# Two layers of a hybrid diffusion backbone on one core: sums of weights issued one step a unit, four columns at the head of the up-projection, and first products that take latents before context

## The chip, the cores and the metric

The kernel runs as one program on one core of a Trainium2 chip. A core has a matrix engine (TensorE, PE in the profile, with its weight loads shown as PEld), a vector engine (VectorE, DVE), an activation engine (ScalarE, ACT), a general engine (GpSimd, POOL) and a synchronising engine (SyncE, SP). SP, ACT and POOL can each issue transfers (DMA), and each issues in its own order. The metric is the device time of one execution in microseconds, the median of several runs.

## The reference, cut to what matters

512 latent tokens and 256 context tokens of width 1024 pass two layers in float32. `setup_inputs` draws the weights; the shapes are those of the constants.

```python
for l in range(DEPTH):                                  # 2
    sh1, sc1, g1, sh2, sc2, g2 = split(silu(c) @ w_ada[l] + b_ada[l], 6)   # for context: c_ctx
    h  = modulate(rms_norm(x,  norm1_g[l]), sh1, sc1)
    hc = modulate(rms_norm(xc, norm1_g[l]), csh1, csc1)
    glu, q, k, v, rq, rk, rv, rg, gates = split(h @ w_in[l] + b_in[l])     # and of hc
    a   = conv_module(glu)                              # depthwise, 31 taps, layer norm, silu
    att = latent_attention(q, k, v, k_c, v_c)           # 8 heads, 2 kv heads
    ret = retention_output(bidir_retention(rq, rk, rv), rg)
    x = x + g1 * (merge_branches(gates, a, att, ret) @ w_out[l])
    x = x + g2 * conv_ffn(modulate(rms_norm(x, norm2_g[l]), sh2, sc2), w_up[l], w_down[l])
    # context tokens: the same weights, not in the last layer
return rms_norm(x, final_norm_g)
```

## The kernel before, in words

Activations lie with features on the partitions and the 768 tokens in the free dimension. Every large product is done in three matmuls: an operand is split into a rounded part `hi` (ACT, line 218 for weights) and a rest `lo` (DVE, line 219), and hi*hi, hi*lo and lo*hi are added up in PSUM. Weights come as tiles of 128 x 1024 through `Stream`: SP loads them into six raw buffers, ACT and DVE split them at most four tiles ahead. Of the eight PSUM banks, four belong to the pool `pd` (`dps()`) and four to `ps` (`ps()`). Nearly all SBUF tiles come from one pool of 45 slots (`S()`); a new tile waits until what used its slot before is done, a transfer included.

The first layer starts in `start` and `first_products`. SP loads x in eight tiles, then the columns of `w_ada` for the first shift and scale in pieces listed by `START` (column, width, number of weight tiles loaded by then). A piece goes through three stages: `go(0, c0)` its matmuls, `go(1, c0)` two transposes and copies on DVE, `go(2, c0)` a small folding matmul and eight small additions on DVE. Piece by piece the normalised, modulated blocks `hh`, `hl` of 128 features become ready (`modulated1`, `modulated2`), and `products` multiplies each by two units of weights (keys and values, then the first queries). Inside `start` the order of PE, ACT and DVE is the order of the code.

A layer's mixers then run by `ORDER`, a list of units: K and Q (keys, queries), R (retention values), A (starts attention, which runs on beside the units), G (glu, for the convolution, which C starts), P (the other retention inputs), T (gates). Attention goes over four pairs of heads and six token tiles; a pair's output `att` is spilled to memory by `spill` after its last tile, and the retention that follows loads the table `ij` into a slot and makes its decay tables of it (lines 916 and 930).

The first layer's up-projection takes seven products in place of eight for each two-by-two block of `w_up` and of the tokens (`up_seven`, `up_order`). For this, sums of weight blocks are needed: S1 = 21 + 22, S3 = 11 + 21, S2 = 11 + S1, S4 = 12 + S2. `make_sums` lets transfers do them: for each of six batches of columns POOL issues four copies in memory and four accumulating transfers, 1 MB each (half of that in the last batch). The first copy of a sum waits for the last matmul that was written out at that point; `SUMAT` names the six units after which one batch each is issued.

Between mixers and up-projection, `last_chunks` does the last four row blocks of `w_out` once for the second half of the tokens and once for the first, and between its chunks steps the generator of `split_tokens`, which normalises the half that is done and makes the operands "11" and "12" of it. The operands S2, S1, S3, 22, S4 need both halves; `up_seven` steps the generator again for them. So that PE has work until "S2" is there, the products "11" and "12" of the first `UPFIRST` columns come first.

Of the kernel before, what the change touches and what calls it, by code (L numbers as in the profile page):

```python
# [18 lines left out]
F32 = mybir.dt.float32  # L19
# [6 lines left out]
P = 128  # L26
# [12 lines left out]
NSUB = 140  # L39
START = ((0, 256, 2), (256, 256, 0), (512, 256, 4), (768, 256, 0))  # L40
ND = 4
# [8 lines left out]
ATTR, RETR, CONVR, ADAR = (1.0, 1.0), (1.4, 1.6), (0.4, 0.4), (0.06, 0.28, 0.4, 0.33)  # L50
SUMAT = ("R1", "G1", "G2", "G3", "P1", "P2")
QLAG = 2
# [6 lines left out]
PEP, DVP, LATE = (4,), (2, 3), (5,)  # L59
NADA = 24 + 8 * len(PEP)  # L60
ROWS = 1552
# [35 lines left out]

UPFIRST = 3
CUTS = ((0, 4), (4, 8), (8, 12), (12, 16), (16, NFF))
# [3 lines left out]
def up_order():  # L103

    first = range(UPFIRST)
    out = [(n, c) for c in first for n in ("11", "12")] + [(n, c) for n in ("S2", "S1", "S3") for c in first]
    for c in range(UPFIRST - 1):
        out += [("22", c), ("S4", c)]
    for c in range(UPFIRST, NFF):
        out += [("11", c), ("22", c - 1), ("S4", c - 1)]  # L110
        if c in CUTAT:
            out.append((CUTAT[c],))
        out += [("12", c), ("S2", c), ("S1", c), ("S3", c)]
    return out + [("22", NFF - 1), ("S4", NFF - 1)]
# [170 lines left out]
class Kern:  # L285
# [92 lines left out]

    def last_chunks(self, key, xs, segs, hold, evac, norm, lead=0, limit=None):

# [23 lines left out]
        for i, hs in enumerate(halves):  # L404
            for j, m in enumerate(range(KC - hold, KC)):
                evac(m, self.dense(None, xs, hs, ws[j]))
                if i == len(halves) - 1:
                    ws[j] = None
                    self.W.release(tiles[j + 1])
                if gen:  # L410
                    for _ in range(1 + KC // hold):
                        next(gen, None)
                self.tick(self.cost)
# [206 lines left out]

    def make_sums(self, b):

        n = len(batches()[b]) * Q
        src = {x: self.io[f"wup{4 * b + i}"] for i, x in enumerate(BLOCKS)}
        for name, base, more in SUMS:
            t = src[name] = self.up_sums[b][name] = self.dram.tile([P, n], F32, name=f"sum{name}_{b}")
            first = self.nc.gpsimd.dma_start(t, src[base], max_dma_last_dim=2048)

            info = mybir.DependencyInfo(mybir.DependencyClass.Sync, mybir.DependencyReason.DATA)
            self.tc.add_manual_dep(first.ins, self.last_mm.ins.name, info, reason="later")  # L630
            for x in more:
                self.nc.gpsimd.dma_start(t, src[x], accum_op=ALU.add, max_dma_last_dim=2048)


    def rstd2(self, pts, name, y=None):
# [501 lines left out]
    def first_products(self, xs, ada):  # L1137
# [9 lines left out]

        def products(k, units=(0, 1)):
            for u in units:
                wh, wl = wb[u][k % 4]  # L1150
                for t in range(n):
                    pt = banks[u][t // 2][:, 256 * (t % 2):256 * (t % 2) + 256]
# [3 lines left out]

        def weights(c):
            self.W.limit = 2 * c + 2
            return [[self.W.next(("w_in", 0, k * P, col), 256) for k in range(4 * c, 4 * c + 4)] for col in (1536, 1024)]

# [5 lines left out]

        for k in range(KC):
            self.sq_add(k, xs[k], ALL, k == KC - 1)
        r = self.S("rstd")
        self.sq_rstd(ALL, r)  # L1170
        go(0, 0)
        go(1, 0)
        go(2, 0)
        banks = [[self.dps() if ND > 3 * u + v else self.ps() for v in range(n // 2)] for u in range(2)]
        t0 = m1(0)
        wb = weights(0)
        m2(t0, 0)
        t1 = m1(1)
        go(0, 256)
        go(1, 256)  # L1180
        m2(t1, 1)
        products(0)
        go(2, 256)
        t2 = m1(2)
        products(1)
        t3 = m1(3)
# [9 lines left out]
        m2(t4, 4)  # L1196
        wb = weights(1)
        go(0, 768)
# [297 lines left out]
    def spill(self, dst, t, w):  # L1496
        self.nc.gpsimd.dma_start(dst[:, :w], t[:, :w])

# [56 lines left out]
    def layer_mixers(self, l, last, segs, T, xs, xsp, first, h2):  # L1555
# [16 lines left out]
        def mixers():  # L1572
# [9 lines left out]
            self.ij = self.S("ij")  # L1582
            nc.gpsimd.dma_start(self.ij[:, :4 * P + 2], io["ij"])
            self.ret_tables()
# [8 lines left out]
        ths, merged = [], [None] * KC  # L1593
        for step in ORDER[l].split():
            kind, i = step[0], int(step[1:] or 0)
# [16 lines left out]
            elif kind == "T":  # L1612
                ths.append(self.gate(2, len(ths), segs))
            if l == 0 and step in SUMAT:
                self.make_sums(SUMAT.index(step))
        self.finish(mix)
# [28 lines left out]
        def evac(m, pts):  # L1645
            for pt, o, c in kinds(pts):
# [6 lines left out]
        return self.last_chunks(lambda m, k: ("w_out", l, k * P, m * P), mm, even(segs), HOLDO[l], evac, norm, LEADO,  # L1653
                                None if l else NUP + UPFIRST)

    def ffn(self, l, h2, xs, segs, T, gen, xsp, xup):
# [57 lines left out]
        def up_seven():  # L1714
# [37 lines left out]
            def s1(c):  # L1752
                Z[c] = (self.ps() if 0 < c < UPFIRST else self.dps())[:, :HALF]
                product(Z[c], "S1", c)
# [29 lines left out]
            for n, x in enumerate(up_order()):  # L1784
# [8 lines left out]
                elif x[0] != "S2" or x[1] >= UPFIRST:  # L1793
                    steps[x[0]](x[1])
                if n == 0:
                    next(gen)
# [194 lines left out]
```

## Time and profile before

| what | value |
|---|---|
| median of 3 runs | 2313.04 us (2312.16 to 2316.35) |
| profiled execution | 2318.38 us |
| its span, first to last instruction | 2316.6 us |
| busy: PE, DVE, ACT, POOL | 96%, 69%, 43%, 6% |
| mean granted clock of PE | 0.988 of 2.4 GHz |
| moved by DMA | 307 MB |

The profiled execution lies 5.3 us above the median of the runs. PE's busy time says only that a matmul was under way; a clock below 1.0 means that matmuls took longer.

### The profile page before, as it was taken

What the parts mean: (1) busy time and instruction counts of PE and PEld (TensorE: products, weight loads), DVE (VectorE), ACT (ScalarE), POOL (GpSimd) and SP (SyncE); (2) the same over time, 40 slices, a digit from 0 to 9 for tenths busy, and PEclk for the clock granted to TensorE, in tenths of its full rate; (3) what the DMA queues carried; (4) which work ended last, traced back from release to release, by engine and by line L of the source; (5) the groups of instructions that cost most, each with busy time, mean ns of one, the idle gap of its engine ahead of it and who ended that gap; (6) DMA issues with size and microseconds to landing.
All of it is one profiled execution on the core that took longest, in us unless ns stands there. A gap on an engine that the chain in (4) does not pass through costs nothing.

```text
span 2316.6 us, 34409 instructions
## 1 busy us (share of the span) xinstructions
PE 2232.2 (96%) x13386; PEld 2037.1 (88%) x13386; DVE 1604.8 (69%) x3219; ACT 989.0 (43%) x1707; POOL 144.5 (6%) x225
## 2 busy tenths in 40 slices
PE   6999968999999989999999989999999999999998
PEld 5988958999999989999999979888887889888887
DVE  6876936889985567565655669878699756744445
ACT  3465643342242346554454434565343434423233
POOL 0001111100010000101101100000001100000000
PEclk9999989999999999999999999999999999999999
DMA  8226894813343333737647521111126623432221
GB/s 304 101 99 173 232 243 126 216 64 117 129 156 128 106 103 100 182 119 191 153 152 183 184 109 56 58 55 58 55 80 222 252 84 111 159 113 97 100 91 37
DMA packets 104466, 307.03 MB, mean 133 GB/s; under 512 B 11024, under 2 KB 13344, under 8 KB 104304
## 3 DMA queue, kind: packets, MB, share of 16 engines
q1 hardware_dynamic: 66240, 186.34, 23.5%
q0 software_dynamic: 38064, 118.50, 18.9%
q8 instruction: 105, 1.72, 0.3%
q14 instruction: 57, 0.47, 0.1%
HBM read 282.26 MB, written 68.68 MB: 151 GB/s over the span
## 4 chain that ended last, share of the span: by engine, by line
PE 53%; issue 3%; DVE 3%; DMA 1%; ACT 1%; POOL 0%; DVEq 0%; POOLq 0%; ACTq 0%
PE pd L319 31%; PE pd L1724 11%; PE ps L319 8%; PE ps L1724 2%; PE ps L1378 1%; DVE wlo L219 1%; DMA crow<-crow 0%; DMA rowa<-wadt 0%; ACT whi L218 0%; DVE cacc L827 0%; DMA rl<-attsp 0%; DVE qq L1326 0%; ACT dx L1805 0%; DMA raw<-wstream 0%; DVE rowa L599 0%
## 5 line engine op out<-in xcount | busy, mean ns | idle before, releaser
L218 ACT ACTIVATE whi<-raw 128x1024 fp32r<-128x1024 f32 x313 | 331.4, 1061 | 748.0 <-PE pd L319 492.0
L219 DVE TENSOR_TENSOR wlo<-raw,whi 128x1024 fp32r<-128x1024 f32 x313 | 382.3, 1222 | 258.8 <-ACT whi L218 245.1
L319 PE MATMUL pd<-hh,whi 128*128 128x384 f32 (+2 forms) x1472 | 471.1, 360 | 0.0
L319 PE MATMUL pd<-hh,wlo 128*128 128x384 f32 (+2 forms) x1472 | 470.2, 359 | 0.0
L319 PE MATMUL pd<-hl,whi 128*128 128x384 f32 (+2 forms) x1472 | 469.5, 359 | 0.0
L319 PEld LDWEIGHTS pd<-hh,whi 128*128 128x128 f32 x1472 | 270.9, 188 | 28.0 <-issue 1.8
L319 PEld LDWEIGHTS pd<-hh,wlo 128*128 128x128 f32 x1472 | 271.4, 188 | 25.9 <-issue 1.1
L319 PEld LDWEIGHTS pd<-hl,whi 128*128 128x128 f32 x1472 | 271.2, 188 | 25.9 <-issue 0.7
L827 DVE SCALAR_TENSOR_TENSOR cacc<-u,vec,cacc 128x497 f32<-128x497 f32 (+9 forms) x360 | 220.9, 650 | 2.0
L1724 PE MATMUL pd<-hh,whi 128*128 128x384 f32 x512 | 171.8, 339 | 9.1 <-ACT hh L716 9.1
L1724 PE MATMUL pd<-hl,whi 128*128 128x384 f32 x512 | 172.3, 336 | 0.5 <-DVE hl L717 0.4
L1724 PE MATMUL pd<-hh,wlo 128*128 128x384 f32 x512 | 171.7, 336 | 0.0
L1361 ACT ACTIVATE prob<-ps,amx,qrs 128x256 f32<-128x256 f32 (+1 forms) x144 | 93.8, 656 | 91.3 <-DVE amx L1356 74.9
L319 PE MATMUL pd<-whi,hl 128*128 128x256 f32 x416 | 120.3, 290 | 5.9 <-DVE hl L784 5.9
L319 PE MATMUL pd<-whi,hh 128*128 128x256 f32 x416 | 120.3, 292 | 2.1 <-ACT hh L781 2.1
L319 PE MATMUL pd<-wlo,hh 128*128 128x256 f32 x416 | 119.3, 287 | 0.0
L319 PE MATMUL pd<-hidh,whi 128*128 128x512 f32 (+1 forms) x302 | 104.1, 356 | 4.0 <-DVE x L1814 4.0
L1724 PEld LDWEIGHTS pd<-hh,whi 128*128 128x128 f32 x512 | 96.5, 189 | 12.0 <-ACT hh L716 10.1
L319 PE MATMUL pd<-hidl,whi 128*128 128x512 f32 (+1 forms) x302 | 103.1, 353 | 0.0
L319 PE MATMUL pd<-hidh,wlo 128*128 128x512 f32 (+1 forms) x302 | 102.9, 354 | 0.0
L599 DVE SCALAR_TENSOR_TENSOR rowa<-rowa,crow 128x768 f32<-128x768 f32 (+1 forms) x144 | 94.4, 686 | 8.9 <-DMA rowa<-wadt 8.9
L588 POOL DMA_DIRECT2D rowa<-wadt x72 | 39.1, 543 | 950.1 <-DVE wlo L219 737.1
(298 smaller groups left out, 4312.1 us busy)
## 6 DMA issues: line engine op xcount, KB each, us to landing
raw<-wstream SPq DMA_DIRECT2D x236, 512.0 KB, 3.5
rowa<-wadt POOLq DMA_DIRECT2D x72, 512.0 KB, 4.3
sumS<-wup POOLq DMA_DIRECT2D x30, 1024.0 KB, 13.0
raw<-sumS SPq DMA_DIRECT2D x88, 256.0 KB, 3.7
raw<-wup SPq DMA_DIRECT2D x66, 256.0 KB, 3.6
xup<-dx POOLq DMA_DIRECT2D x32, 384.0 KB, 7.2
sumS<-sumS POOLq DMA_DIRECT2D x10, 1024.0 KB, 9.7
adar<-wada SPq DMA_DIRECT2D x16, 384.0 KB, 7.6
```

Source lines behind the costliest of these rows:

```text
L218: nc.scalar.activation(hi, r, AF.Copy)
L219: nc.vector.tensor_tensor(lo, r, hi.bitcast(F32), op=ALU.subtract)
L319: self.last_mm = self.nc.tensor.matmul(out, w, x, start=start, stop=stop)
L588: nc.gpsimd.dma_start(loaded[-1], self.io["wadt"][l, 8 * pc + c])
L599: nc.vector.scalar_tensor_tensor(out, raw[:, a:b], 1.0, t[:, o:o + b - a], op0=ALU.mult, op1=ALU.mult, accum_out=acc[:, c, j, h:h + 1])
L827: nc.vector.scalar_tensor_tensor(acc[:, a:b], u[:, a + d:b + d], w(k), acc[:, a:b], op0=ALU.mult, op1=ALU.add)
L1361: nc.scalar.activation(pr[:, o - k0:o - k0 + c], pt[:, :c], AF.Exp, scale=rs, bias=mx[:, 2:3], accum_out=sm[:, j:j + 1])
L1378: nc.tensor.transpose(pt[:, b * P:b * P + P], pr[:, o + b * P:o + b * P + P], self.ident)
L1724: nc.tensor.matmul(pt, w[:, b], x, start=start and k == 0 and i == 0, stop=k == 3 and i == 2, skip_group_check=not start)
```

## The change

`START` begins with two pieces of 128 columns in place of one of 256. `first_products` makes the sum of squares, the reciprocal root and the first block separately for latents and for context, and the first unit's products of the latents come before everything of the context. `make_sums(n)` is called after every unit from the ninth on (G1) and issues for each batch the step that is its turn: the copies, then S1 and S3, then S2, then S4; every transfer of a step waits for the last matmul written out. `spill` issues on ACT instead of POOL, the load of `ij` on SP instead of POOL. `UPFIRST` becomes 4, all products "11" come before all "12", Z of all four columns lies in `ps`, the generator is stepped after the second product, and `PACE` steps it 3, 3, 1 and 1 times behind the four last chunks.

```diff
-START = ((0, 256, 2), (256, 256, 0), (512, 256, 4), (768, 256, 0))
+START = ((0, 128, 2), (128, 128, 0), (256, 256, 4), (512, 256, 0), (768, 256, 0))
-SUMAT = ("R1", "G1", "G2", "G3", "P1", "P2")
+SUMFROM = 8
-UPFIRST = 3
+PACE = (3, 3, 1, 1)
+UPFIRST = 4
-    out = [(n, c) for c in first for n in ("11", "12")] + [(n, c) for n in ("S2", "S1", "S3") for c in first]
+    out = [(n, c) for n in ("11", "12", "S2", "S1", "S3") for c in first]
...
-                    for _ in range(1 + KC // hold):
+                    for _ in range(pace[j] if pace else 1 + KC // hold):
...
-    def make_sums(self, b):
...
+    def make_sums(self, n):
+        steps = ((), ("S1", "S3"), ("S2",), ("S4",))
+        for b in range(len(batches())):
+            if not 0 <= n - b < len(steps):
+                continue
+            for name, base, more in SUMS:
+                if n == b:
+                    t = sums[name] = self.dram.tile([P, len(batches()[b]) * Q], F32, name=f"sum{name}_{b}")
+                    ops.append(nc.gpsimd.dma_start(t, src[base], max_dma_last_dim=2048))
+                elif name in steps[n - b]:
+                    for x in more:
+                        ops.append(nc.gpsimd.dma_start(sums[name], src[x] if x in src else sums[x], accum_op=ALU.add,
+                                                       max_dma_last_dim=2048))
+            for op in ops:
+                self.tc.add_manual_dep(op.ins, self.last_mm.ins.name, info, reason="later")
...
-        for k in range(KC):
-            self.sq_add(k, xs[k], ALL, k == KC - 1)
-        r = self.S("rstd")
-        self.sq_rstd(ALL, r)
-        go(0, 0)
+        for k in range(KC - 1):
+            self.sq_add(k, xs[k], ALL)
+        for seg in ALL:
+            self.sq_add(KC - 1, xs[KC - 1], [seg])
+        for (o, c), in (lat, ctx):
+            y.append(self.ps()[:, :c])
+            self.mm(y[-1], self.ones, self.sq[:, o:o + c], True, True)
+            if o == 0:
+                go(0, 0)
         go(1, 0)
+        self.rstd2([(y[0], *lat[0])], "rstd", r)
         go(2, 0)
...
+        t0 = self.modulated1(0, xs[0], r, 0, 0, lat)
+        wb = [weights(0, 0)]
+        self.modulated2(0, t0, 0, 0, lat, h0)
+        wb.append(weights(0, 1))
+        products(0, (0,), th)
+        self.rstd2([(y[1], *ctx[0])], "rstd", r)
+        t0 = self.modulated1(0, xs[0], r, 0, 0, ctx)
+        self.modulated2(0, t0, 0, 0, ctx, h0)
+        go(0, 128)
+        products(0, (1,), th)
+        go(1, 128)
+        products(0, (0,), tc)
+        go(2, 128)
         t1 = m1(1)
+        products(0, (1,), tc)
+        m2(t1, 1)
         go(0, 256)
         go(1, 256)
-        m2(t1, 1)
-        products(0)
+        products(1, (0,))
         go(2, 256)
         t2 = m1(2)
-        products(1)
+        products(1, (1,))
...
     def spill(self, dst, t, w):
-        self.nc.gpsimd.dma_start(dst[:, :w], t[:, :w])
+        self.nc.scalar.dma_start(dst[:, :w], t[:, :w])
...
-            nc.gpsimd.dma_start(self.ij[:, :4 * P + 2], io["ij"])
+            nc.sync.dma_start(self.ij[:, :4 * P + 2], io["ij"])
...
-            if l == 0 and step in SUMAT:
-                self.make_sums(SUMAT.index(step))
+            if l == 0 and n >= SUMFROM:
+                self.make_sums(n - SUMFROM)
...
-                Z[c] = (self.ps() if 0 < c < UPFIRST else self.dps())[:, :HALF]
+                Z[c] = (self.ps() if c < UPFIRST else self.dps())[:, :HALF]
...
-                if n == 0:
+                if n == 1:
                     next(gen)
```

## Rows read from the trace of the kernel before

**Rows 1.** The page: span, and each engine's busy time.

```profile
span 2316.6 us, 34409 instructions
PE 2232.2 (96%) x13386; PEld 2037.1 (88%) x13386; DVE 1604.8 (69%) x3219; ACT 989.0 (43%) x1707; POOL 144.5 (6%) x225
```

**Rows 2.** PE's waits over the span: total us, times, longest.

```profile
PE ps L319 <- ACT probt L1379: 23.9, 1, 23.9
...
PE pd L1724 <- ACT hh L716: 9.1, 3, 6.7
```

**Rows 3.** Windows: each engine's busy us, granted clock, DMA share, GB/s.

```profile
327.90:351.80 23.90, 0.01 (x2) 0.01 (x2) 0.00 (x0) 0.45 (x3) 4.26 (x6) 0.56 0.96 253
351.80:355.00 3.20, 3.20 (x20) 2.87 (x21) 0.00 (x0) 1.21 (x5) 1.24 (x3) 0.53 0.68 95
361.40:364.90 3.50, 0.05 (x3) 0.03 (x1) 2.47 (x7) 3.50 (x10) 0.00 (x0) 1.00 0.00 0
364.90:370.00 5.10, 5.10 (x30) 4.82 (x31) 3.65 (x7) 0.22 (x1) 0.00 (x0) 0.67 0.00 0
```

**Rows 4.** Timeline of ACT and POOL: start, us, instruction, idle before and releaser.

```profile
296.02 0.30 ACT L1393 ACTIVATE att<-ps 128x128 f32<-128x128 f32 x1
...
337.75 0.96 POOL L1497 DMA_DIRECT2D attsp<-att  x1
...
351.35 0.38 ACT L1379 ACTIVATE probt<-ps 128x256 f32<-128x256 f32 x1 [24.87 <-DMA attsp<-att]
351.50 0.99 POOL L1583 DMA_DIRECT2D ij<-ij  x1
```

**Rows 5.** Timeline behind the stall; weight loads 232 to 327 (ns min/median/max, first, last).

```profile
361.00 0.49 ACT L916 ACTIVATE kdec<-lg,ij 128x8 f32<-128x8 f32 x2 [6.91 <-DMA ij<-ij]
...
364.90 1.59 PE L319 MATMUL ps<-rq,rk 64*128 64x128 f32 x8 [3.45 <-DVE kb L981]
...
L199 SPq DMA_DIRECT2D raw<-wstream x7: 327/328/328, 236.5 to 320.3; - x7
```

**Rows 6.** Transfers issued 232 to 327: size, median us to landing.

```profile
raw<-wstream SPq DMA_DIRECT2D x7, 512.0 KB, 7.3
attsp<-att POOLq DMA_DIRECT2D x1, 384.0 KB, 13.2
```

**Rows 7.** The second load of `ij`; sums, by tile (first and last start).

```profile
1583.16 0.54 POOL L1583 DMA_DIRECT2D ij<-ij  x1 [5.24 <-PE ps L1378]
...
L632 POOL DMA_DIRECT2D sumS<-sumS x12: 874/1042/1440, 194.4 to 456.1; - x12
...
L197 SPq DMA_DIRECT2D raw<-sumS x88: 319/327/922, 800.7 to 1285.1; - x88
```

**Rows 8.** Timeline at the up-projection's head; last row: one product in the chain.

```profile
849.92 0.61 DVE L1648 SCALAR_TENSOR_TENSOR x<-pd,coef,x 128x384 f32<-128x384 f32 x1
...
855.68 0.51 ACT L657 ACTIVATE sqt<-x 128x384 f32<-128x384 f32 x1
...
858.40 0.55 DVE L1737 TENSOR_TENSOR fg<-fg,ps 128x384 f32<-128x384 f32 x1
...
860.27 1.22 DVE L219 TENSOR_TENSOR wlo<-raw,whi 128x1024 fp32r<-128x1024 f32 x1
...
869.16 1.33 PE L1724 MATMUL pd<-hh,whi 128*128 128x384 f32 x3 [6.66 <-ACT hh L716]
...
875.78 0.45 PE L1724 MATMUL pd<-hh,whi 128*128 128x384 f32 x1 [1.15 <-ACT hh L716]
...
901.00 2.08 PE ps L1724 x12
```

**Rows 9.** The start: a wait of PE, a piece's matmuls, matmuls with ones.

```profile
PE pd L319 <- DVE hl L784: 4.5, 2, 2.3
...
24.10 2.52 PE L319 MATMUL ps<-adar,cc 128*32 128x256 f32 x32
...
L319 PE MATMUL ps<-sqt,ones 128*128 128x512 f32 x2 | 1.9, 1061 | 0.0
```

More of the change, by code (lines that the diff above doesn't have):

```diff
@@ L59 @@
 PEP, DVP, LATE = (4,), (2, 3), (5,)
-NADA = 24 + 8 * len(PEP)
+NADA = 26 + 8 * len(PEP)
 ROWS = 1552
@@ L377, in dense, with last_chunks @@
         return pts
-    def last_chunks(self, key, xs, segs, hold, evac, norm, lead=0, limit=None):
+    def last_chunks(self, key, xs, segs, hold, evac, norm, lead=0, limit=None, pace=None):
         n = len(xs)
@@ L619, in up_operand @@
         return t[:, j * Q:j * Q + Q]
-    def make_sums(self, b):
[L623 to L632, printed above, removed]
+    def make_sums(self, n):
+        nc = self.nc
+        info = mybir.DependencyInfo(mybir.DependencyClass.Sync, mybir.DependencyReason.DATA)
+        steps = ((), ("S1", "S3"), ("S2",), ("S4",))
+        for b in range(len(batches())):
+            if not 0 <= n - b < len(steps):
+                continue
+            sums = self.up_sums[b]
+            src = {x: self.io[f"wup{4 * b + i}"] for i, x in enumerate(BLOCKS)}
+            ops = []
+            for name, base, more in SUMS:
[8 more added lines that the diff above has]
+                self.tc.add_manual_dep(op.ins, self.last_mm.ins.name, info, reason="later")
     def rstd2(self, pts, name, y=None):
@@ L1146, in go, with products @@
                     next(part)
-        def products(k, units=(0, 1)):
+        def products(k, units=(0, 1), ts=range(n)):
             for u in units:
                 wh, wl = wb[u][k % 4]
-                for t in range(n):
+                for t in ts:
                     pt = banks[u][t // 2][:, 256 * (t % 2):256 * (t % 2) + 256]
@@ L1155, in products, with weights @@
                         self.mm(pt, x, y, k == 0 and i == 0 and t % 2 == 0, k == KC - 1 and i == 2 and t % 2 == 1)
-        def weights(c):
-            self.W.limit = 2 * c + 2
-            return [[self.W.next(("w_in", 0, k * P, col), 256) for k in range(4 * c, 4 * c + 4)] for col in (1536, 1024)]
+        def weights(c, u):
+            self.W.limit = 2 * c + u + 1
+            return [self.W.next(("w_in", 0, k * P, (1536, 1024)[u]), 256) for k in range(4 * c, 4 * c + 4)]
         m1 = lambda k: self.modulated1(0, xs[k], r, 0, k, ALL)
@@ L1165, in m2 @@
             self.modulated2(0, t, 0, k, ALL, self.h[k])
-        for k in range(KC):
-            self.sq_add(k, xs[k], ALL, k == KC - 1)
-        r = self.S("rstd")
-        self.sq_rstd(ALL, r)
-        go(0, 0)
+        for k in range(KC - 1):
+            self.sq_add(k, xs[k], ALL)
+        for seg in ALL:
+            self.sq_add(KC - 1, xs[KC - 1], [seg])
+        r, y = self.S("rstd"), []
+        lat, ctx = ([seg] for seg in ALL)
+        th, tc = range(SEQ // P), range(SEQ // P, n)
+        h0 = (self.S("hh", F32R), self.S("hl", F32R))
+        for (o, c), in (lat, ctx):
[3 more added lines that the diff above has]
+                go(0, 0)
         go(1, 0)
+        self.rstd2([(y[0], *lat[0])], "rstd", r)
         go(2, 0)
         banks = [[self.dps() if ND > 3 * u + v else self.ps() for v in range(n // 2)] for u in range(2)]
-        t0 = m1(0)
-        wb = weights(0)
-        m2(t0, 0)
+        t0 = self.modulated1(0, xs[0], r, 0, 0, lat)
+        wb = [weights(0, 0)]
+        self.modulated2(0, t0, 0, 0, lat, h0)
+        self.h.append(h0)
+        wb.append(weights(0, 1))
[8 more added lines that the diff above has]
+        go(2, 128)
         t1 = m1(1)
+        products(0, (1,), tc)
+        m2(t1, 1)
         go(0, 256)
         go(1, 256)
-        m2(t1, 1)
-        products(0)
+        products(1, (0,))
         go(2, 256)
         t2 = m1(2)
-        products(1)
+        products(1, (1,))
         t3 = m1(3)
@@ L1196, in first_products @@
         m2(t4, 4)
-        wb = weights(1)
+        wb = [weights(1, u) for u in range(2)]
         go(0, 768)
@@ L1593, in layer_mixers @@
         ths, merged = [], [None] * KC
-        for step in ORDER[l].split():
+        for n, step in enumerate(ORDER[l].split()):
             kind, i = step[0], int(step[1:] or 0)
@@ L1653, in layer_mixers @@
         return self.last_chunks(lambda m, k: ("w_out", l, k * P, m * P), mm, even(segs), HOLDO[l], evac, norm, LEADO,
-                                None if l else NUP + UPFIRST)
+                                None if l else NUP + UPFIRST, None if l else PACE)
     def ffn(self, l, h2, xs, segs, T, gen, xsp, xup):
```

## The prediction

> **What bounds the kernel now.** I began with the page: the span and what lies around it are the base of every sum below, and TensorE (PE) is busy in 96% of it [rows 1]. So 84 us is all that can be won without taking matmuls away, and the question is where these 84 us lie and which of them the change touches. The list of PE's waits says that [rows 2]: one single wait of 23.9 us, put down to ScalarE (ACT) writing `probt`, and 9.1 us on `hh` tiles, in three pieces. The stretch around the long wait shows that it is no wait of PE on ACT alone [rows 3]: from 327.9 to 351.8 PE, VectorE (DVE) and ACT all stand, while the DMA engines are 96% busy, and PE's granted clock falls to 0.56. The reader is to see a whole core waiting for a transfer.
>
> Which transfer is told by putting ACT's and GpSimd's (POOL's) rows in one order [rows 4]. The third pair of heads has its last output in `att` at 296.3. Its spill to memory is an issue on POOL, and that issue starts at 337.75: for 41 us it stood in POOL's queue behind the copies and accumulations of `make_sums`, each of which waits for the one before it to land. ACT's next `probt` needs a buffer and got it only when the spill had landed; it starts at 351.35 after 24.87 us of idling "DMA attsp<-att". Directly behind, the load of `ij` is issued on POOL at 351.50, and the retention tables wait for it.
>
> **The change, part by part.**
>
> *Spill on ACT's queue, `ij` on SP's, sums one step a unit.* The spill no longer has POOL's queue ahead of it. ACT writes `att` itself, so at 296.3 the spill is next in ACT's own order and waits only for ACT's last write. Behind it stands all of ACT's work, but what it costs there is an issue: 0.33 us by the issues on SP [rows 5], eight in the program, 2.6 us of an engine busy 43% of the span [rows 1]; I cost it at nothing. If the cover were gone, 2.6 us is the price. The spill that was issued among the sums before took 13.2 us to land [rows 6]; by that price this one lands at 310, and ACT asks for the buffer at 326.5 (351.35 less 24.87). So the wait goes whole: 23.9 us. With it goes the slow clock behind it: 3.2 us at 0.53 [rows 3], 1.5 us of matmul time. Together 25.4 us. Since all three compute engines stood, no hidden work is uncovered by this.
>
> The next thing late is `ij`. Before, PE lost 3.45 us waiting for `kb`, which needs the tables, which waited 6.91 us for `ij` [rows 5]; then 5.1 us passed at 0.67 of the clock [rows 3], another 1.7 us. In all 5.1 us. On SP, `ij` stands among the weight loads; SP issued one at 320.3 and none again until after the attention [rows 5], so it can go out between 320.3 and 326.6, whichever buffer it waits for. Landing took 9.5 us (351.50 to 361.0). Issued at 320.3 it lands at 329.8 and the 5.1 us are won; issued at 326.6 it lands at 336.1, which is the old place shifted by 24.87, and nothing is won. I take the middle, 2.6 us, and keep 0 and 5.1. In layer 1 `ij` waited 5.24 us on POOL for a buffer [rows 7]; on SP that holds up the weight loads behind it by as much. They have the weights already split and two loads in flight as cover; a tile was loaded every 14 us there [rows 5], so I cost it at nothing, and at 5.2 us if the cover fails, less than the first rival below costs.
>
> The sums themselves are the same 48 transfers. Before, the last was issued at 456 [rows 7]; now the first may start only after unit G1 instead of R1, and the last after the second T, by when the old kernel was done with them. They are first read at 800.7 [rows 7]. That is over 300 us of slack, so I cost their delay at nothing. What their closer packing does to the weight stream is a rival below.
>
> *Four columns in the head of the up-projection, a slower pace of the normalisation.* After the last `w_out` matmuls PE has six products ("11" and "12" of three columns) until "S2" is ready. It ran out at 862.5, waited 6.66 us, did the first half of three "S2" products and waited 1.15 us more [rows 8]. From 862.5 to 875.78 are 13.3 us, in which 18 matmuls ran; a product of 12 takes 2.08 us [rows 8], so 3.1 us of work: 10.2 us lost, the slow clock in between included (it hides nothing, since the second `hh` was the limit). The change has eight products, 4.2 us more cover, and the half "S2" is 24 matmuls, 4.2 us instead of 3.1. With the chain of `hh` unmoved, 13.3 - 4.2 - 4.2 = 4.9 us are lost, a gain of 5.3. The chain moves too. Earlier: the last chunk's `x` was written at 850.5, but ACT squared it only at 855.68, behind the block of "12" that the old pace puts first [rows 8]; the new pace puts one step of it behind. That gives 5 us at most, and 1 us if DVE's own order keeps the `hl` of that block ahead of the rstd. Later: one more addition of a "12" product, 0.55 us, and perhaps one more weight split, 1.22 us, on DVE [rows 8]. So 5.3 + 1 - 1.8 = 4.5 to 5.3 + 5 - 0.5 = 9.8 us; the third piece of the `hh` waits, 1.3 us later on, can go too. I keep 4.5 and 10. I take 7, near the middle. All eight PSUM banks are now held by X and Z; the fourth Z must wait for the last "12" to be added, which DVE does four products earlier, so I cost that at nothing.
>
> *The first layer's start.* PE's steady work begins with the `hl` of latents alone. It gains at most what PE waited for `hl`, 4.5 us [rows 9], and half of the matmuls with ones (1.9 us for latents' second half [rows 9]) leave PE. Against this: the second piece of modulation, whose matmuls ran 24.10 to 26.6 in the shadow of that wait [rows 9], now comes after the first products, 2.5 us; and DVE, which sets the pace here, has the small steps of one more piece and one more addition of squares. For a gain stand 4.5 and 1.9, against it 2.5 and what DVE's chain lengthens, for which no row is near. I take 0 and keep 3 us either way, about the size of the 2.5 us that comes into view.
>
> **The sum.** 25.4 + 2.6 + 7 + 0 = 35.0 us, out of the profiled execution's 2318.4: 2283.4. The median of the runs is 5.3 us below that execution; the parts are the same there, so 2313.0 - 35 = 2278. I say 2279.
>
> The Trainium skill speaks against the first part. Its page "DMA: Bandwidth & Descriptors", section "Issuing engines are not separate DMA queues", says that transfers from any issuing engine run on the same 16 DMA engines and that another issuer saves only the issuing time, usually small beside the transfer. By that rule the moved spill would be late all the same. The trace differs: 41 us of this spill's delay lay before its issue and 13.6 after it [rows 4]; by the rule the sum would hold the 7 us of the up-projection alone, by the rows it holds 35.
>
> **The rivals.**
>
> *The wait goes to another transfer.* The fourth spill leaves at about 329 and `ij` at 327, both now under the sums' traffic, which had ended for a while when they went out before. At 13.2 us each [rows 6] they land at 342 and 340. If retention's first tiles need either, PE stands from 336.6 (361.4 less 24.87) to about 346 (`kb` came 3.9 us behind `ij` [rows 5]), 9 us, and the slow clock after it costs 2: 11 in place of 5.1, so 6 lost instead of 2.6 won. That gives 25.4 - 6 + 7 = 26 us, 2287; a second such wait brings 2297. For it: DMA is 96% busy there [rows 3]. Against: the weights of SP landed in 7.3 us in the same traffic [rows 6]. Chance 0.12.
>
> *It does not do what it says: the DMA engines, not the queue, made the spill late.* Then moving it changes only its issue, the wait stays, and the up-projection's 7 us are all: 2306. Against it the 41 us before the issue. This is what the rule named above would give. Chance 0.05.
>
> *The other side: the sums starve the weights.* With a step of up to eight transfers in each unit the DMA engines are full from G1 to the second T without the pauses of before. Weight tiles landed in 7.3 us beside the sums, one every 14 us [rows 5, 6], and some 16 are loaded in those 220 us. Above 14 us landing, each microsecond costs up to 16; at 16.2 us the 35 are gone, and from there the kernel is slower: at 17 us 16 x 3 - 35 = 13 slower, 2326. It needs the landing to more than double. Chance 0.03.
>
> **How the numbers follow.** The forecast as reckoned has 0.80, the rivals 0.12, 0.05, 0.03. Low end: 25.4 + 5.1 + 10 + 3 = 43.5, 2269; high end of the forecast: 25.4 + 0 + 4.5 - 3 = 27, less the 1.5 us if the clock dips anyway, 2288. The range reaches into the first rival, 2296, and 2 us below the low end since the ends were summed from rough orders: 2267 to 2296. About 0.2% (4.6 us) is what can be told from no change; faster is the forecast, the first rival and most of the second: 0.94; same 0.03, slower 0.03.
>
> **What would show it.** Right: no wait over 5 us on `probt`; PE's clock at 1.0 from 320 to 350; the spill's issues as ACT's; the sums ending near 450; PE's waits on `hh` in the up-projection 2 to 5 us in place of 9.1; the first `hl` wait earlier, but the K and Q0 products ending within 3 us of the old place. Wrong: ACT or DVE idling on "DMA attsp" or "DMA ij" around 330 to 345, weight loads landing in over 12 us with PE waiting on `wlo`, or new waits on `ps` banks at "S1".

## The result, and the profile after

The changed kernel takes 2287.70 us (median of 4 runs, 2286.72 to 2288.21). The kernel before took 2313.11 in the same comparison; the ratio is 0.9887, 95% interval 0.987 to 0.9904. Forecast were 2279 and a range of 2267 to 2296. A ratio here is estimated from all fast runs of both kernels, so it is not exactly the quotient of the two medians. The profiled execution took 2287.4 us, 31.0 less than the one before it; the medians are only 25.4 apart.

The page of the kernel after (engine, busy us, share of the span), to be read against [rows 1]:

```profile
span 2285.4 us, 34466 instructions
...
PE 2228.8 (98%) x13418; PEld 2037.6 (89%) x13418; DVE 1608.4 (70%) x3235; ACT 988.8 (43%) x1708; POOL 138.2 (6%) x215
```

PE's waits over the span of the kernel after (line, total us, times, longest), to be read against [rows 2]:

```profile
PE ps L320 <- DVE sq L672: 16.0, 1, 16.0
PE pd L320 <- ACT hh L792: 7.0, 3, 4.9
PE pd L1756 <- ACT hh L727: 5.7, 3, 2.1
...
PE ps L320 <- DVE kb L992: 2.1, 6, 0.5
PE pd L1756 <- DVE wlo L220: 2.0, 1, 2.0
PE pd L1756 <- ACT whi L219: 1.1, 1, 1.1
```

The 23.9 us on `probt` are gone, and no piece of the wait on `kb` is over 0.5. Two waits are new, on `wlo` and `whi`, the split weights. The longest wait left, 16.0 us ahead of the first matmul with ones, stood in the kernel before too, second in its list:

```profile
PE ps L319 <- DVE sq L661: 14.7, 1, 14.7
```

The stretch of the old stall in the kernel after (busy us of each engine, PE's clock, DMA share, GB/s), against [rows 3]:

```profile
326.00:352.00 26.00, 25.91 (x212) 23.45 (x211) 18.22 (x44) 8.36 (x24) 6.70 (x8) 1.00 0.91 178
352.00:370.00 18.00, 18.00 (x105) 17.95 (x105) 14.33 (x25) 8.68 (x12) 6.08 (x7) 1.00 1.04 309
```

PE works through, at a granted clock of 1.00, beside DMA engines about as busy as before (0.91 and 1.04, against 0.96). Now the two moved transfers in the kernel after: ACT's timeline around the third spill, SP's around `ij`, and ACT's first use of `ij`.

```profile
297.30 0.29 ACT L1425 ACTIVATE att<-ps 128x128 f32<-128x128 f32 x1
297.62 0.33 ACTq L1529 DMA_DIRECT2D attsp<-att  x1
```

```profile
307.94 13.83 SPq L200 DMA_DIRECT2D raw<-wstream  x2
323.06 0.33 SPq L1615 DMA_DIRECT2D ij<-ij  x1
```

```profile
330.96 0.49 ACT L927 ACTIVATE kdec<-lg,ij 128x8 f32<-128x8 f32 x2 [0.40 <-ACT att L1425]
```

The spill leaves right behind the last `att`, against 41 us later in [rows 4]; `ij` leaves 28.4 us earlier than in [rows 4], and the tables wait for `att` and no transfer ([rows 5]: 6.91 us on `ij`).

From the same instructions in both traces, the time the changed kernel is ahead:

| place | before | after | ahead, us |
|---|---|---|---|
| first matmul with ones | 14.66 | 16.03 | -1.4 |
| `hl` that ends the start's last wait (PE) | 58.09 | 60.70 | -2.6 |
| an `att` before the stall | 323.53 | 324.70 | -1.2 |
| a `sg` behind it | 393.97 | 365.09 | 28.9 |
| last `w_out` block added to x | 849.92 | 821.03 | 28.9 |
| first `dx` of the second down product issued to be added (POOL) | 1040.90 | 1011.17 | 29.7 |
| end | 2316.6 | 2285.4 | 31.2 |

So 30.1 us came from the stall (28.0 forecast), 0.8 from the head of the up-projection (7 forecast), and the start cost 2.6 (0 forecast), of which 1.4 were back before the stall. The last 1.5 us arise behind the second down product's start; no run takes them apart.

### The profile page after: what moved, and what is told of

It reads as the page before. It is cut to its first block, busy times and chain, and to the rows that moved or that the text cites. A ratio compares the mean times of both kernels' runs of the same rounds, so it can differ in the third digit from the quotient of the medians.

```text
span 2285.4 us, 34466 instructions
## 1 busy us (share of the span) xinstructions
PE 2228.8 (98%) x13418; PEld 2037.6 (89%) x13418; DVE 1608.4 (70%) x3235; ACT 988.8 (43%) x1708; POOL 138.2 (6%) x215
## 3 DMA queue, kind: packets, MB, share of 16 engines
q1 hardware_dynamic: 66816, 186.87, 23.8%
## 4 chain that ended last, share of the span: by engine, by line
PE 88%; DVE 5%; issue 4%; ACT 1%; DMA 1%; POOL 0%; SPq 0%; DVEq 0%; POOLq 0%; ACTq 0%
PE pd L320 58%; PE ps L320 14%; PE pd L1756 11%; PE ps L1756 3%; PE ps L1410 2%; DVE wlo L220 1%; ACT whi L219 1%; DVE cacc L838 0%; PE ps L1323 0%; DMA x<-xt 0%; DMA rowa<-wadt 0%; DVE ht L783 0%; DVE sq L672 0%; DVE qq L1358 0%; DVE mod L544 0%
## 5 line engine op out<-in xcount | busy, mean ns | idle before, releaser
L1756 PE MATMUL pd<-hh,whi 128*128 128x384 f32 x496 | 166.8, 340 | 6.8 <-ACT hh L727 5.7
L1756 PE MATMUL pd<-hh,wlo 128*128 128x384 f32 x496 | 167.0, 337 | 2.0 <-DVE wlo L220 2.0
L1756 PE MATMUL pd<-hl,whi 128*128 128x384 f32 x496 | 167.1, 337 | 0.5 <-DVE hl L728 0.4
```

The costliest lines, as they stand in the source:

```text
L1756: nc.tensor.matmul(pt, w[:, b], x, start=start and k == 0 and i == 0, stop=k == 3 and i == 2, skip_group_check=not start)
```

## The experiments

Each was timed beside the kernel before, whose medians there were 2315.2 to 2316.8. Four chips were used: one for e1, e2, e3 and e6, one for e5, e7, e8 and e9, one for e10, e11 and e13, one for e14; beside the changed kernel the kernel before had 2313.1. Medians of different groups are therefore to be compared by their ratios. The intervals of the ratios are 0.001 to 0.002 to either side, so 2 to 5 us; differences below that are read from the traces, and said to be so.

| run | what | median us | ratio (95%) | span us |
|---|---|---|---|---|
| e1_spill | before + spill on ACT | 2317.19 | 1.0006 (0.9995 to 1.0017) | 2314.5 |
| e3_sums | before + sums one step a unit | 2316.43 | 1.0002 (0.9993 to 1.001) | 2315.0 |
| e2_queues | before + spill on ACT, ij on SP | 2287.90 | 0.9886 (0.9871 to 0.9901) | 2289.3 |
| e6_sums_queues | e2 + sums one step a unit | 2287.01 | 0.9885 (0.9871 to 0.9898) | 2284.0 |
| e7_nohead | after, old head | 2289.37 | 0.9885 (0.9864 to 0.9905) | 2286.5 |
| e5_nostart | after, old start | 2282.99 | 0.9856 (0.9835 to 0.9877) | 2280.0 |
| e8_oldpace | e5, old pace | 2283.32 | 0.9855 (0.9834 to 0.9876) | 2281.3 |
| e9_three | e5, three columns | 2284.12 | 0.9864 (0.9843 to 0.9885) | 2279.2 |
| e13_piece | after, first piece of 256 | 2285.00 | 0.9865 (0.9851 to 0.988) | 2281.0 |
| e10_early | e5, operands earlier | 2282.18 | 0.9852 (0.9833 to 0.9871) | 2275.5 |
| e11_five | e5, five split buffers | 2287.32 | 0.9873 (0.9857 to 0.989) | 2285.9 |
| e14_both | e10, five split buffers | 2295.00 | 0.9909 (0.9888 to 0.993) | 2296.7 |

**Which part removed the stall.** Four kernels take the three edits of the attention apart.

e1_spill:

```diff
     def spill(self, dst, t, w):
-        self.nc.gpsimd.dma_start(dst[:, :w], t[:, :w])
+        self.nc.scalar.dma_start(dst[:, :w], t[:, :w])
```

> The kernel before with one line changed: the spill of attention issues on ACT; the load of ij stays on POOL, the sums stay as they were. Theory (POOL's order was the cause, and whatever still stands in it stays late): the wait on probt goes whole, but ij still stands on POOL behind the sums that came ahead of the old spill, which cleared at 337.75; it lands about 9.5 us later, 347.3, and the tables follow 3.9 us behind. PE needs them at 336.6, so about 14.6 us of the 25.4 come back as a wait for kb: 11 to 14 us faster in the profile. Rival (the DMA engines were full, not the queue): the spill lands as late as before, within 3 us of no change.

No gain at all. PE's and POOL's timelines of e1_spill:

```profile
361.13 1.59 PE L319 MATMUL ps<-rq,rk 64*128 64x128 f32 x8 [24.22 <-DVE kb L981]
```

```profile
334.53 1.02 POOL L632 DMA_DIRECT2D sumS<-sumS  x1 [2.02 <-DMA sumS<-wup]
335.18 1.02 POOL L627 DMA_DIRECT2D sumS<-wup  x1
348.50 1.00 POOL L632 DMA_DIRECT2D sumS<-sumS  x1 [12.30 <-DMA sumS<-wup]
349.13 0.96 POOL L1583 DMA_DIRECT2D ij<-ij  x1
```

The spill is no longer waited for, and PE waits 24.22 us for `kb` instead of 23.9 for `probt`. One more accumulation stands ahead of `ij` than I had counted; it waits 12.3 us for the transfer before it, so `ij` leaves at 349.13 and not at 337.75. ACT, whose next work needs it, stood 27.2 us. The 11 to 14 us expected did not come, since that chain was one transfer short. The rival (full DMA engines) is not borne out either: the three spills of this stretch landed in 5.4 to 7.0 us, and none was late.

e2_queues adds the second line:

```diff
-            nc.gpsimd.dma_start(self.ij[:, :4 * P + 2], io["ij"])
+            nc.sync.dma_start(self.ij[:, :4 * P + 2], io["ij"])
```

> The kernel before with the spill on ACT and ij on SP; the sums stay as they were, each accumulation waiting on POOL for the transfer before it. Theory (POOL's order): both waits go, 28 to 30.5 us in the profile, 24 to 30 us of medians, all that the changed kernel gained and a little more, because the changed start (2.7 us longer in its profile) is not in it. Rival (the spacing of the sums did it, since the DMA engines were 96% busy): less than half of that, under 13 us, with ACT or DVE still idling on attsp or ij.

2287.9, a ratio of 0.9886 against 0.9887: these two lines are worth as much as the whole change, with the sums as crowded as before. `ij` on SP with the spill left on POOL was not run; that the wait on `probt` would then have stayed is argued from [rows 4] only.

e3_sums has `SUMFROM`, the new `make_sums` and its call, and nothing else:

```diff
-            if l == 0 and step in SUMAT:
-                self.make_sums(SUMAT.index(step))
+            if l == 0 and n >= SUMFROM:
+                self.make_sums(n - SUMFROM)
```

> The kernel before with the sums one step a unit; spill and ij stay on POOL. Theory: in the changed kernel no POOL issue waits for another transfer of the sums to land (its idle times before them end on PE), so POOL's queue no longer blocks and the spill goes out at about 297 even on POOL. It then lands behind up to 7 MB of sums that were issued at 287 to 293, about 27 us by the 259 GB/s of that stretch, at 322 or so; ACT asks at 326.5. So 20 to 30 us in the profile, 15 to 28 of medians: either part alone would have removed most of the stall. Rival (only the move to other queues counts): the third spill stands behind the sums as before, a wait of over 15 us stays on probt and the gain is under 8 us.

I expected most of the gain, and there is none. Timelines of e3_sums, POOL, then ACT, then PE:

```profile
294.43 0.56 POOL L1507 DMA_DIRECT2D attsp<-att  x1 [4.43 <-ACT att L1403]
325.44 2.13 POOL L640 DMA_DIRECT2D sumS<-sumS  x2 [30.44 <-PE ps L319]
326.74 2.92 POOL L640 DMA_DIRECT2D sumS<-wup  x2
327.99 4.20 POOL L637 DMA_DIRECT2D sumS<-wup  x4
335.82 0.56 POOL L1507 DMA_DIRECT2D attsp<-att  x1 [3.63 <-DMA sumS<-sumS]
342.25 0.55 POOL L1593 DMA_DIRECT2D ij<-ij  x1 [5.87 <-issue]
```

```profile
366.04 0.49 ACT L926 ACTIVATE kdec<-lg,ij 128x8 f32<-128x8 f32 x2 [22.71 <-DMA ij<-ij]
```

```profile
368.80 1.15 PE L319 MATMUL pd<-hh,whi 128*128 128x384 f32 x2 [26.21 <-ACT rk L1446]
```

As expected the third spill leaves at once. But `ij` is issued behind a whole step of the sums, eight transfers of up to 1 MB, and lands 23.8 us after its issue. The spills show the same, with a pair that can be compared: the landing of the third spill, issued right behind the same step of the sums, first in e3_sums (by POOL at 294.43), then in the kernel after (by ACT at 297.62):

```profile
DMA to landing us min/median/max: 27.0/27.0/27.0
```

```profile
DMA to landing us min/median/max: 7.4/7.4/7.4
```

So freeing POOL's issues was not enough. Behind a whole step of the sums in POOL's queue a transfer landed in 23.8 and 27.0 us. It is not POOL's queue as such: in e1_spill, where the sums waited for one another and only one of them was issued right ahead of it, `ij` landed in 8.1 us by POOL, as in e2_queues by SP (8.0).

e6_sums_queues has all three edits of the attention, the sums one step a unit and both moved transfers, without the new start and head:

> The kernel before with the sums one step a unit, the spill on ACT and ij on SP: the changed kernel without its start and without its head of the up-projection. Theory from the two traces (start costs 2.7 us at first and about 1.2 after the sums' place is gained back, head worth about 0.9): 25 to 28 us of medians, within 2 us of the changed kernel and of the run with the queues alone. By the prediction's terms (head worth 7, start 0) it would be 7 us slower than the changed kernel: a gain of 18 us of medians.

2287.0. Beside the moved queues the spacing of the sums has no effect that these runs can tell (e2_queues 2287.9), and this kernel is not 7 us slower than the changed one but level with it.

**The head of the up-projection and the start.** e5_nostart and e7_nohead are the changed kernel without one of the two.

```diff
 e5_nostart:
-START = ((0, 128, 2), (128, 128, 0), (256, 256, 4), (512, 256, 0), (768, 256, 0))
+START = ((0, 256, 2), (256, 256, 0), (512, 256, 4), (768, 256, 0))
...
 e7_nohead:
-UPFIRST = 4
+UPFIRST = 3
...
```

> The changed kernel with the start of before (one first piece of 256 columns, latents and context together). Theory from the traces: the changed start reaches the keys 2.7 us late and 1.2 us of that are still there at 324, so this kernel is 1.2 to 2.7 us faster than the changed one (2287.7): 2285 to 2286.5. By the prediction (start worth 0) it is 2287.7. Against the run with sums and queues alone (2287.0) it shows the head of the up-projection: by the prediction 7 us faster, 2280; by the traces of up to 2 us, since 7.3 us are won at S2 and most are lost again 30 to 80 us later.

> The changed kernel with the head of the up-projection of before (three columns, old order, old pace). Theory from the traces: head worth 2, so 2288.5 to 2290; it is the slowest of this call if the start costs 1 to 3 and the head brings 2. By the prediction (head worth 7): 2294.7.

The four kernels make two pairs for each part, but the medians do not decide them. By medians the head is worth 4.0 us with the old start (e6 to e5) and 1.7 with the new one (e7 to after), and the start costs 4.7 (e5 to after) and 2.4 (e6 to e7). Only e5 and e7 ran beside one another, though. By the ratios (e6 0.9885, e5 0.9856, e7 0.9885, after 0.9887) the head is worth 0.0029 with the old start and nothing with the new one, and the start costs 0.0031 with the new head and nothing with the old one. The traces tell more.

For the start, take the first `qsq` of the keys on DVE. It comes at 79.2 to 84.4 with the old start (eleven executions, 81.6 on average) and at 85.1 and 85.2 with the new one. The spread goes with the clock granted to PE from 30 to 60: in the three executions with the old start that had 1.00 there (e5, e9, e10) `qsq` comes at 79.2 to 79.8, and the trace of before, 82.5, had 0.91. The new start had 1.00 (after) and 0.98 (e7). At an equal clock it is 5.3 to 6 us late, twice what the two traces of before and after show. DVE's timeline of e5_nostart, then of the kernel after:

```profile
79.75 0.36 DVE L1281 TENSOR_TENSOR qsq<-kraw,cs 128x64 f32<-128x64 f32 x2
```

```profile
85.21 0.36 DVE L1302 TENSOR_TENSOR qsq<-kraw,cs 128x64 f32<-128x64 f32 x2
```

For the head, take the time from the last `w_out` block to the first `dx` of the second down product. With the old head it is 190.6 to 194.7 us (before, e1, e2, e3, e6, e7; 192.3 on average), with four columns and the new order 190.1 to 190.6 (after, e5, e8, e13; 190.4 on average): some 2 us won, between 0 and 4.6 from one pair of executions to another. PE's timeline of e6_sums_queues, and that of the kernel after, at the first two halves of "S2":

```profile
836.22 1.33 PE L1734 MATMUL pd<-hh,whi 128*128 128x384 f32 x3 [6.66 <-ACT hh L726]
842.84 0.79 PE L1734 MATMUL pd<-hh,whi 128*128 128x384 f32 x3 [1.88 <-ACT hh L726]
```

```profile
839.22 0.97 PE L1756 MATMUL pd<-hh,whi 128*128 128x384 f32 x4 [1.70 <-ACT hh L727]
840.61 0.44 PE L1756 MATMUL pd<-hl,whi 128*128 128x384 f32 x1 [0.42 <-DVE hl L728]
846.24 0.96 PE L1756 MATMUL pd<-hh,whi 128*128 128x384 f32 x4 [1.88 <-ACT hh L727]
...
869.75 1.49 PE L1756 MATMUL pd<-hh,whi 128*128 128x384 f32 x4 [2.08 <-ACT hh L727]
...
915.17 0.44 PE L1756 MATMUL pd<-hh,whi 128*128 128x384 f32 x1 [1.10 <-ACT whi L219]
917.82 0.69 PE L1756 MATMUL pd<-hh,wlo 128*128 128x384 f32 x1 [2.02 <-DVE wlo L220]
```

At S2 the waits fall from 8.5 us to 4.0, and the slow clock beside them goes as well. Windows of e6_sums_queues, then of the kernel after (PE's busy us, clock, DMA share, GB/s):

```profile
833.00:850.00 17.00, 11.64 (x54) 0.82 0.24 68
```

```profile
836.00:853.00 17.00, 12.96 (x70) 1.00 0.26 84
```

Then 2.08 are lost ahead of the first product "22", and 3.1 at 914 to 918. The granted clock is 0.91 from 864 to 882 and 0.87 from 912 to 925.

e8_oldpace and e9_three:

```diff
 e8_oldpace:
-PACE = (3, 3, 1, 1)
+PACE = (3, 3, 3, 3)
 e9_three:
-UPFIRST = 4
+UPFIRST = 3
```

> The run without the changed start, with the pace of the normalisation of before (three steps behind each of the last chunks). Theory (the pace brings S2's operands forward, since the last chunk's square does not stand behind the block of 12): the square of the last chunk starts some 4 us later behind its x, PE waits 2 to 4 us longer for the first S2, and the time is 2 to 4 us above the run without the changed start. Rival (the pace is idle, the cover of the fourth column does all): within 1 us of it.

> The run without the changed start, with three columns in the head in place of four (the new order and pace stay). Two products of cover and one half product less: PE waits about 5 us longer at S2. Theory (four columns at S2 hold all four buffers of split weights, and what PE loses at 867 to 921 comes from there): these later losses of some 7 us shrink to the 3 of the run with the old head, so the time is within 2 us of the run with four columns. Rival (the later losses have another cause, the order in which operands and splits are written out): they stay, and it is 4 to 5 us slower.

The pace is idle: 0.3 us, and PE waits the same 1.70 us at the first S2. Three columns cost 1.1 us, which the interval cannot tell from nothing; PE waits 5.25 us at S2 in place of 1.70, and of the later losses the wait before "22" goes, while 2.4 us on `whi` and `wlo` stay. The theory's numbers came out (within 2 us, later losses down to 2.4 and 1.4 on `dx`), its cause is not shown: with three columns PE is held up 3.6 us longer at S2, and the others' work may simply have been ready by then. The rival, 4 to 5 us slower, did not come.

e10_early writes the operands "22" and "S4" out two products before the first "22":

```diff
+                if n + 2 < len(order) and order[n + 2][0] == "22":
+                    while "S4" not in ready:
+                        ready.add(next(gen))
```

> The run without the changed start, with the operands 22 and S4 written out two products before their first use (in front of S3 of the third column) in place of at it. Theory (what is won at S2 is given back where the other engines' work is written out too late; the wait of 2.08 us before the product 22 and the slow clock behind it, 1.7, are such a place): that wait goes, and the time is 2 to 3.8 us below the run without the changed start (2283.0). Rival (the stretch from S2 to the end of the first down product is bound by ACT and DVE together, so what is won at one place is lost at the next): within 1 us of it, and the waits on whi and wlo at 905 to 912 grow.

Windows of e10_early, PE only (busy us, clock, DMA share, GB/s), and the same of e5_nostart, where the product "22" starts at 864.29 after its 2.08 us:

```profile
856.00:880.00 24.00, 24.00 (x140) 1.00 0.38 118
900.00:920.00 20.00, 16.00 (x87) 1.00 0.62 165
```

```profile
856.00:880.00 24.00, 21.80 (x116) 0.93 0.33 108
900.00:920.00 20.00, 16.87 (x86) 0.91 0.55 153
```

The loss before "22" is gone, its slow clock too, and the stretch up to the second down product takes 186.0 us, 4.3 less than in e5. At the down product PE loses 4.0 us in place of 3.1: less on `whi` and `wlo` (2.1), but 1.9 on `dx`. The profiled executions differ by as much as the stretch (2275.5 against 2280.0). The medians do not show it: 2282.2 against 2283.0, and the four runs of e10 lie between 2277.6 and 2286.6. By its median it is the fastest version here; that it beats e5 is open.

e11_five gives the split weights a fifth buffer, at the cost of two raw ones:

```diff
-RAWB, RAWS = 2, 6
+RAWB, RAWS = 2, 4
-WB = 4
+WB = 5
```

> The run without the changed start, with five buffers of split weights in place of four, and four raw buffers in place of six, everywhere. Theory (the later loss, 3.1 us of waits on whi and wlo at the first down product and a slow clock behind them, comes from splits that wait for PE to free one of four buffers): these waits go, 3 to 4.5 us faster than 2283.0. Rival (ACT and DVE have no time for the splits earlier, or the loads with four raw buffers come late instead): no gain, or slower by waits on whi that end on DMA.

PE's waits from 860 to 935 in e11_five:

```profile
PE pd L1735 <- ACT hh L727: 2.1, 1, 2.1
...
PE ps L320 <- ACT dx L1816: 0.2, 1, 0.2
PE pd L1735 <- DVE wlo L220: 0.2, 1, 0.2
```

Of the 3.1 us on `whi` and `wlo` 0.2 are left, and the stretch takes 187.7 us, 2.6 less than in e5: the splits did wait for a buffer. But the last `w_out` block comes 4.5 us later than in e5, and the median is 4.3 higher, though the intervals overlap. 4.0 us of that arise up to the first `qsq` (83.8 against 79.8). Windows of PE there (busy us, clock, DMA share, GB/s), of e5_nostart, then of e11_five:

```profile
30.00:60.00 30.00, 27.66 (x261) 1.00 0.70 256
```

```profile
30.00:60.00 30.00, 27.65 (x238) 0.90 0.51 195
```

PE is busy for as long but got through fewer matmuls, at a lower clock. e2_queues, with the old buffers, had the same clock there (0.90) and the same delay (83.8), so the buffers need not be the cause. Why all four runs of e11_five lie above 2286 stays open.

e13_piece is the changed kernel with the first piece 256 columns wide again (`START` and `NADA`, the number of blocks it is stored in, as before) and no `go(…, 128)`:

> The changed kernel with the first piece of modulation 256 columns wide again, so that no second piece of 128 stands between the first block and the second; latents still go before context. Theory (the second piece in DVE's chain is what the changed start costs: the second block's hl comes at 36.8 in place of 32.3): that hl is back at 32.5 to 34 and the time at 2283 to 2285, 3 to 4.7 us below the changed kernel (2287.7). Rival (the split of latents and context costs: the seventh addition of squares puts the first matmul with ones 1.0 to 1.4 us later, and the reciprocal root is done in two chains): the time stays within 1.5 us of 2287.7.

DVE's timeline at the second block's `hl`, first e5_nostart, then the kernel after (with the modulation piece ahead of it), then e13_piece:

```profile
32.28 1.14 DVE L795 SCALAR_TENSOR_TENSOR hl<-ht,mod,hh 128x512 fp32r<-128x512 f32 x2
```

```profile
33.46 0.66 DVE L544 TENSOR_TENSOR mod<-ps,vec 32x2 f32<-32x2 f32 x4 [1.56 <-PE ps L320]
...
36.79 1.15 DVE L795 SCALAR_TENSOR_TENSOR hl<-ht,mod,hh 128x512 fp32r<-128x512 f32 x2 [0.40 <-ACT hh L792]
```

```profile
33.58 1.15 DVE L795 SCALAR_TENSOR_TENSOR hl<-ht,mod,hh 128x512 fp32r<-128x512 f32 x2 [0.46 <-ACT hh L792]
```

3.2 of the 4.5 us come back there, and the first `qsq` comes at 81.7 at a clock of 0.99, so 3.5 of the 5.5 us. By the medians 2.7 of 4.7 come back, which the intervals cannot tell from nothing. The rest, by what is left of the edit, is the split of latents and context: the eighth square is now added on DVE, and the first matmul with ones comes at 15.3 to 16.0 in place of 14.6 to 15.2.

e14_both joins e10 and e11, with five raw buffers in place of six and 44 slots in place of 45:

> The run with the operands 22 and S4 written out earlier, and in it five buffers of split weights, five raw buffers in place of six, and 44 slots in place of 45. Theory (the two later losses of the head add up, and each goes by its own remedy): no wait on hh before the product 22 and none on whi or wlo at the first down product; from the last w_out block to the second down product 2 us less than with the earlier operands alone, and a time of 2278 to 2282, if five raw buffers keep the start as it was. Rival (buffers taken from the loads and the slots cost as much elsewhere, as four raw buffers did at the start, 4 us): 2283 or more.

The rival holds: 2295.0, its six runs between 2286.6 and 2301.1, and the head's stretch takes 190.2 us, 4.2 more than in e10. The waits on `whi` and `wlo` are down to 0.3 us, but PE's waits between 880 and 1260 are, in e14_both:

```profile
PE ps L320 <- ACT dx L1820: 13.8, 9, 6.3
PE pd L1735 <- DVE wlo L220: 0.3, 1, 0.3
```

e10_early has 1.9 us of the first kind. ACT's idle time ahead of `dx` ends on transfers of earlier `dx` tiles, 19.2 us against 4.8, which points at slots being short for them. Whether the one slot or the one raw buffer did it was not taken apart.

## Why the prediction was right, and where its terms were off

**Spill and `ij` (25.4 + 2.6 = 28.0 forecast, 30.1 measured).** The mechanism was right: the transfers were late in POOL's queue. I had costed `ij` at the middle, 2.6, and it brought the upper end, 5.1. It did leave in the middle of my window, at 323.06; but I had given it the 9.5 us to its first use that it had had on POOL, by which it would have come at 332.6, 1.6 us after ACT was ready for it (330.96). On SP it landed in 3.5 us. That the whole 5.1 came is luck by that sum: the landing that made it so was not reckoned, and in e2_queues it was 8.0, and ACT waited 0.48 us for `ij`. What I had not seen is that the two lines depend on one another: I had booked 25.4 for the spill and 2.6 for `ij`, and by e1_spill the spill alone gives nothing, since `ij` would have been late by as much. The sum was near (2.1 us short), its split was wrong. The first rival, in which `ij` and the fourth spill land late under the sums' traffic, did not come: all of these landed in at most 8.5 us in e2 and in the kernel after.

**The sums (nothing forecast, nothing measured).** e2 against e6. The rival in which they starve the weights did not come: from 233 to 475 the weight tiles landed in 7.0 us (e2), 7.4 (e6) and 7.5 (after) by the median, where the rival needed over 14.

**By the Trainium skill.** The Trainium skill's page "DMA: Bandwidth & Descriptors", section "Issuing engines are not separate DMA queues", read as I read it, would have had the wait stay, 2306. e2_queues measures the contrary, a gain of 1.1% from two lines that change only the issuing engine. Whether transfers of different issuers share the engines, as the Trainium skill says there, no run here tests. In this kernel the cost lay in what stood ahead in the issuer's order (e1_spill) and in the queue itself (a spill issued right behind the same step of the sums: 27.0 us to land by POOL, 7.4 by ACT).

**The head (7 forecast, 0.8 by the two traces, some 2 by all of them): this term failed.** Its steps for S2 held: four columns cut the waits there from 8.5 to 4.0 us and the slow clock with them. The waits on `hh` over the whole up-projection came to 5.7 us, just outside the 2 to 5 named as the sign, since one of 2.08 ahead of "22" is new. What failed is the silence about what comes next: I had stopped at S2. PE, ahead by the 4.5 us of waits and the slow clock, met the operands "22", written out only at their first use, and then splits that waited for a buffer. e10 and e11 remove one each, and the stretch gives 4.3 and 2.6 us more (one execution each). The 1 to 5 us that I gave the pace were not there (e8).

**The start (0 with 3 either way forecast): its size was off.** The two traces show 2.6 us, inside the bounds, but the one of before had a clock of 0.91 from 30 to 60 and the one after 1.00; against the old start at 1.00 the cost is 5.3 to 6 us, outside them. I had set the gain at `hl` against the second piece on PE. The piece's cost lies on DVE's chain, with a wait for PE in it, 3.2 us by e13_piece; and with the added square on DVE the longest wait of the start, which [rows 2] leave out, went from 14.7 to 16.0.

**From profile to median.** I took the 5.3 us between the profiled execution and the median of before as the same for both kernels. The changed kernel has no such difference (2287.4 and 2287.7), and on the chips of the experiments before's medians were 2315.2 to 2316.8. Without that subtraction the forecast would have been 2283.4, 4 us off and not 9. From span to span the parts gave 31.2 us for the 35.0 forecast: 2.1 too little on the stall, 6.2 too much on the head, 1.2 too much on the start, and 1.5 nobody forecast. So the forecast holds by its largest term; the head, its second term, hardly came.

## What to carry to other kernels

Before costing a transfer that is moved out of a queue, list everything late that the queue still holds: the next one can give back the whole gain. When a wait is removed from the engine that sets the pace, follow that engine to the next places where others' work is written out just in time, and price them before booking the gain. Cutting the first piece smaller brought the first product forward here and nothing behind it; count the fixed steps of the extra piece on the engine whose chain they join.

## What I had not expected of the hardware

Two things. A transfer of 384 KB behind the same sums landed in 7.4 us by ACT's queue and in 27.0 us by POOL's, with the DMA engines full in both kernels (a share of 1.0 and more while they were under way). And the same old start ends up to 5 us apart in different executions and on different chips (79.2 to 84.4), with a granted clock of 1.00 to 0.89 from 30 to 60; a difference of that size between two single profiles cannot be put down to an edit before the clocks have been compared.
